# Expert stage of a hybrid transformer block: combining products one pair later, the first pair's rows fetched alone, the last pair evacuated in halves

## The chip, the cores and the metric

The kernel runs as one program on one core of a Trainium2 chip. The metric is the device time of one execution in microseconds (us). A profiled execution gives the trace: its span runs from the first to the last instruction, and a little time lies around the span.

## The reference, cut to what matters

The program computes a first block with two mixers, then a second block with a sparse-attention mixer and a mixture of experts, then a norm. Only the mixture of experts is touched here. Each of 512 tokens is routed to 2 of 32 experts; every expert is a gated two-layer network.

```python
def run(args):                                   # xb: the rows of one expert
    xb, e = args
    gate, up = jnp.split(xb @ w_gate_up[e], 2, axis=-1)
    return (jax.nn.silu(gate) * up) @ w_down[e]
...
y = jax.ops.segment_sum(y_buf[dest] * w_s[:, None].astype(h.dtype), tok_s, num_segments=n_tok)
```

`w_gate_up[e]` is 1024 x 512 and `w_down[e]` is 256 x 1024, in 32-bit floats: 3 MB for each expert, all of which has to be read once.

## The kernel before, in words

All of this is in `moe`. **Routing** works on 128 partitions by 4 token tiles: `rs` is the inverse norm of a token, `rk` its rank within its expert, `Wd` its weight. `wr` holds, for each pair of experts, the weights, `rs` and the token numbers, split into a high and a low part (a copy on ScalarE, a subtraction on VectorE: `split`, lines 328 and 329). `rkT` is `rk` transposed.

**Slots.** Each expert has 64 slots, so a pair of experts fills 128 partitions. There are 16 pairs, j = 0 to 15, in 8 groups of two, g = 0 to 7.

- `prepare(g)` builds a 0/1 matrix `P` on VectorE (L1956), multiplies it with `wr` (L1961) to get the token number and the weights of each slot, turns the numbers into indices `ix` (L1966), and gathers the rows of the tokens from device memory with two indirect DMAs on GpSimd (L1969), one for each pair. `s3`, `w` and `r` (L1972 to L1976) are small sums and copies on GpSimd.
- `turn(j)` transposes the gathered rows in two halves of four 128 x 128 blocks on TensorE (L1994) through one PSUM bank, `ga`, and scales them into `Xs`, alternating ScalarE and VectorE (L1983, L1981).
- `gate_up(j)` multiplies with the weights of the two experts (L2011). Each expert uses a 64-column half of the array, and the two halves run side by side when their calls alternate. ScalarE evacuates the result into `G` (L2013).
- `act(j)` transposes `G` (L2020) and applies the gate (L2022 to L2025), giving `H`.
- `down(j)` multiplies `H` with the second weights into `dn` (L2034), again one half of the array for each expert, and evacuates 128 x 1024 numbers as a high part `yh` on ScalarE (L2037) and a low part `yl` on VectorE (L2038). It also builds `PT`, the matrix that sends slots back to tokens (L2041, L2043).
- `combine(g)` is a generator of eight groups (4 token tiles x 2 column halves). Each group has four products, `yh` and `yl` of two pairs (L2052), in one of two `cb` banks, and one addition into `acc` on VectorE (L2055).

**Order.** For pair j the loop issues `gate_up(j)`, the first half of `turn(j + 1)`, `down(j - 1)`, the second half of `turn(j + 1)`, four combining groups, and `act(j)`. The groups of pairs 2g and 2g + 1 begin in the iteration whose `down` is that of pair 2g + 1. This order is only a priority: a planner, which runs the program against its own costs, fixes the order of the instructions on each engine, and it may put later work in where earlier work isn't ready by its reckoning. Within an engine the order so fixed is then kept on the chip. `tc.issue_after(x)` puts the instructions of a block behind `x` on `x`'s own engine.

**Weights** are streamed by SyncE's queue into a ring of buffers of 1 MB, about 12 of them in this stage; a buffer is loaded again when its last product is done.

**End.** `down(15)` is followed by all eight groups of the last two pairs, and `last_norm` squares on ScalarE, scales on VectorE (L2097) and stores. `overflow` handles experts with over 64 tokens: its few small VectorE instructions (L2108 to L2120) count them, and its loop does not run here.

Of the kernel before, what the change touches and what calls it, by code (L numbers as in the profile page):

```python
# [10 lines left out]
FT = mybir.dt.float32  # L11
FR = mybir.dt.float32r
BF = mybir.dt.bfloat16
I32 = mybir.dt.int32
AF = mybir.ActivationFunctionType
# [5 lines left out]
D = 1024  # L21
# [304 lines left out]
def split(k, raw, hi, lo, lo_eng=None):  # L326
    nc = k.nc
    nc.scalar.copy(hi, raw)
    (lo_eng or nc.vector).tensor_tensor(lo, raw, hi.bitcast(FT), OP.subtract)
# [1457 lines left out]
def moe(k, A, C, out, ctx, mhp, mh, ml):  # L1787
# [36 lines left out]
    with tc.tile_pool(name="mo1", bufs=2, reuse_waits="tile") as wk, tc.tile_pool(name="mo1x", bufs=1, reuse_waits="tile") as xp, \  # L1824
# [99 lines left out]
            nc.tensor.matmul(rp[:, 4], oneb, asg[:, u], start=(u == 0), stop=(u == 3))  # L1924

        nc.vector.tensor_scalar(rk, asg, -1000.0, 1000.0, op0=OP.mult, op1=OP.add)
        nc.vector.tensor_tensor(rk, rk, rp[:, 0:4], OP.add)
        nc.vector.tensor_copy(cnt, rp[:, 4])
        d, r = tiny(1, "d"), tiny(1, "r")
        nc.vector.tensor_tensor(d, m2, m1, OP.subtract)  # L1930
# [4 lines left out]
        nc.vector.tensor_tensor(Wd, o1, r.to_broadcast(b32), OP.mult)  # L1935
        nc.vector.tensor_tensor(o2, o2, d.to_broadcast(b32), OP.mult)
        nc.vector.tensor_tensor(Wd, Wd, o2, OP.add)
        wp = Wd.rearrange("p t (j e) -> p t j e", e=2)
        split(k, wp, wr[:, :, :, 0:4:2], wr[:, :, :, 1:4:2])
        rsb = rs[:, :, None].to_broadcast([128, 4, N_PAIR])  # L1940
        split(k, rsb, wr[:, :, :, 4], wr[:, :, :, 5])
        tr = pp.tile([128, 512], FT, name="pg", bufs=2)
        for i in range(4):
            nc.tensor.transpose(tr[0:32, i * 128:i * 128 + 128], rk[:, i], k.ident)
# [4 lines left out]
    with tc.tile_pool(name="mo2", bufs=2, reuse_waits="tile") as wk, tc.tile_pool(name="mo2y", bufs=1, reuse_waits="tile", side="right") as yp, \  # L1949
# [3 lines left out]
        def prepare(g):  # L1953

            P = wk.tile([128, 4, 4, 64], FR, name="P", bufs=1)
            nc.vector.tensor_tensor(P, rk[:, :, 4 * g:4 * g + 4, None].to_broadcast([128, 4, 4, 64]),  # L1956
                                    iota[:, None, None, :].to_broadcast([128, 4, 4, 64]), OP.is_equal)
            sp = pp.tile([128, 2, 8], FT, name="cb", bufs=2)
            for j in range(2):
                for t in range(4):  # L1960
                    nc.tensor.matmul(sp[:, j], P[:, t, 2 * j:2 * j + 2].rearrange("p e s -> p (e s)"),  # L1961
                                     wr[:, t, 2 * g + j], start=(t == 0), stop=(t == 3))
            s8 = wk.tile([128, 2, 8], FT, name="s8")
            nc.vector.tensor_copy(s8, sp)
            ix = wk.tile([128, 2], I32, name="ix")
            nc.vector.tensor_copy(ix, sp[:, :, 6])  # L1966
            for j in range(2):
                x = XG[2 * g + j] = wk.tile([128, D], FT, name="xg", bufs=3)
                nc.gpsimd.indirect_dma_start(out=x, out_offset=None, in_=xd[:, :],  # L1969
                                             in_offset=bass.IndirectOffsetOnAxis(ap=ix[:, j:j + 1], axis=0))  # L1970
            s3 = wk.tile([128, 2, 3], FT, name="s3")
            nc.gpsimd.tensor_tensor(s3, s8[:, :, 0:6:2], s8[:, :, 1:6:2], OP.add)  # L1972
            w, r = (wk.tile([128, 2], FT, name=n, bufs=3) for n in ("sw", "sr"))
            for i, a in enumerate((slice(0, 64), slice(64, 128))):
                nc.gpsimd.tensor_copy(w[a], s3[a, :, i])
            nc.gpsimd.tensor_copy(r, s3[:, :, 2])  # L1976
            SW[g] = (w, r)

        def scaled(x, v, kk):
# [21 lines left out]
        def gate_up(j):  # L2001

            g, i = divmod(j, 2)
            ps = pp.tile([128, 512], FT, name="gu", bufs=2)
            xs = Xs.pop(j)
            for c in range(2):
                ws = [k.W.get_raw() for _ in HALF]
                for a in range(4):
                    kk = 4 * c + a
                    for o, w in zip(HALF, ws):  # L2010
                        nc.tensor.matmul(ps[o], xs[:, kk, o], w[:, a], start=(kk == 0), stop=(kk == 7))  # L2011
            G[j] = wk.tile([128, 512], FT, name="G")
            nc.scalar.activation(G[j], ps, AF.Copy, scale=SW[g][1][:, i:i + 1])  # L2013

        def act(j):

            tp = pp.tile([128, 4, 128], FT, name="T")
            x = G.pop(j)
            for f in range(4):
                nc.tensor.transpose(tp[:, f], x[:, 256 * (f // 2) + f % 2:256 * (f // 2) + 256:2], k.ident)  # L2020
            th = wk.tile([128, 2, 128], FT, name="th")
            nc.scalar.activation(th, tp[:, 0:2], AF.Tanh, scale=0.5)  # L2022
            nc.vector.scalar_tensor_tensor(th, th, 1.0, tp[:, 0:2], op0=OP.add, op1=OP.mult)
            H[j] = wk.tile([128, 2, 128], FT, name="H")
            nc.vector.scalar_tensor_tensor(H[j], th, 0.5, tp[:, 2:4], op0=OP.mult, op1=OP.mult)  # L2025

        def down(j):
            ps = pp.tile([128, 2, 512], FT, name="dn")
            h = H.pop(j)
            ws = [k.W.get_raw() for _ in HALF]  # L2030
            for a in range(2):
                for i in range(2):
                    for o, w in zip(HALF, ws):
                        nc.tensor.matmul(ps[o, i], h[:, a, o], w[:, a, 512 * i:512 * i + 512], start=(a == 0), stop=(a == 1))  # L2034
            w = SW[j // 2][0][:, j % 2:j % 2 + 1]
            yh, yl = (yp.tile([128, 2, 512], FR, name=n, bufs=3) for n in ("yh", "yl"))
            nc.scalar.activation(yh, ps, AF.Copy, scale=w)  # L2037
            nc.vector.scalar_tensor_tensor(yl, ps, w, yh.bitcast(FT), op0=OP.mult, op1=OP.subtract)  # L2038
            Y[j] = (yh, yl)
            b = pp.tile([128, 512], FT, name="cb", bufs=2)  # L2040
            nc.tensor.matmul(b, sel[:, 2 * j:2 * j + 2].rearrange("p e s -> p (e s)"), rkT, start=True, stop=True)  # L2041
            PT[j] = yp.tile([128, 512], FR, name="PT", bufs=3)
            nc.vector.tensor_scalar(PT[j], b, col64, None, op0=OP.is_equal)  # L2043

        def combine(g):
            for t in range(4):
                for i in range(2):
                    ps = pp.tile([128, 512], FT, name="cb", bufs=2)
                    n = 0
                    for j in (2 * g, 2 * g + 1):  # L2050
                        for y in Y[j]:
                            nc.tensor.matmul(ps, PT[j][:, t * 128:t * 128 + 128], y[:, i], start=(n == 0), stop=(n == 3))  # L2052
                            n += 1
                    a = acc[:, t, 512 * i:512 * i + 512]
                    nc.vector.tensor_tensor(a, a, ps, OP.add)  # L2055
                    yield

        def steps(g, n):
            for _ in range(n):
                next(g, None)  # L2060
# [4 lines left out]
        for j in range(N_PAIR):  # L2065
            g, i = divmod(j, 2)
            if i == 0 and g + 1 < NG:
                prepare(g + 1)
            gate_up(j)
            nxt = turn(j + 1) if j + 1 < N_PAIR else iter(())  # L2070
            steps(nxt, 1)
            if j:
                down(j - 1)
            if i == 0 and g:
                comb = combine(g - 1)
            steps(nxt, 2)
            steps(comb, 4)
            act(j)
        for _ in comb:
            pass  # L2080
        down(N_PAIR - 1)
        for _ in combine(NG - 1):
            pass


    with tc.tile_pool(name="mo3", bufs=2, reuse_waits="tile") as wk:
        gf = wk.tile([128, D], FT, name="gf", bufs=1)
        nc.scalar.dma_start(gf, A["norm_final_2"].rearrange("(o d) -> o d", o=1).to_broadcast([128, D]))

        def last_norm():  # L2090
            ss, rf = wk.tile([128, 4], FT, name="ss", bufs=1), wk.tile([128, 4], FT, name="rf", bufs=1)
            for t in range(4):
                s = wk.tile([128, D], FT, name="s", bufs=4)
                nc.scalar.activation(s, acc[:, t], AF.Square, accum_out=ss[:, t:t + 1])
                nc.vector.tensor_scalar(ss[:, t:t + 1], ss[:, t:t + 1], 1.0 / D, EPS, op0=OP.mult, op1=OP.add)
                nc.gpsimd.tensor_tensor(rf[:, t:t + 1], ss[:, t:t + 1], k.mhalf, OP.pow)
                nc.vector.scalar_tensor_tensor(s, acc[:, t], rf[:, t:t + 1], gf, op0=OP.mult, op1=OP.mult)  # L2097
                nc.sync.dma_start(out[0, t * 128:t * 128 + 128], s)
        last_norm()
        overflow(k, A, rt, cm, rk, Wd, rs, cnt, xd, acc, last_norm)  # L2100


def overflow(k, A, rt, cm, rk, Wd, rs, cnt, xd, acc, last_norm):

    nc, tc = k.nc, k.tc
    iota, ids, tok = cm[:, 0:64], cm[:, 193:201], cm[:, 201:205]
    x = rt.tile([128, 32], FT, name="ovx")
    nc.vector.tensor_scalar(x, cnt, 64.0, None, op0=OP.is_gt)  # L2108
    for j in range(2, 8):
        nc.vector.scalar_tensor_tensor(x, cnt, 64.0 * j, x, op0=OP.is_gt, op1=OP.add)  # L2110
    ci = x
# [125 lines left out]
```

## Time and profile before

| what | us |
|---|---|
| three runs | 2397.03, 2403.26, 2406.48 (median 2403.26) |
| the profiled execution | 2399.58 |
| its span | 2397.8 |
| busy: TensorE (PE) / VectorE (DVE) / ScalarE (ACT) / GpSimd (POOL) | 2258.6 / 1536.0 / 1068.5 / 710.5 |
| from the first store of normed rows to the first product with expert weights | 2043.5 to 2068.3 |
| first product with expert weights to the last addition | 2068.3 to 2386.5 |

A busy PE is one with a matmul under way by a modelled end; it is not PE at its peak. In the rows below PE is TensorE's matmuls and L with a number is a line of the kernel. "x16" counts records: one call of `gate_up` or `down` gives two, one combining product gives one.

### The profile page before, as it was taken

The numbers are of one execution on the slowest core, as the hardware profiler recorded it, in microseconds if no ns is written. First come the engines' busy times: TensorE is split into PE (matmuls) and PEld (weight loads), VectorE is DVE, ScalarE is ACT, GpSimd is POOL, SyncE is SP. The second block draws the span as 40 slices with busy tenths as digits, with TensorE's granted clock in tenths as the row PEclk, the third lists the DMA queues.
The fourth block names the chain that finished last, engine by engine and source line by source line (L and its number), as shares of the span: only waits on it lengthen the run. The fifth ranks groups of instructions, "written<-read, shape, count | busy, mean of one in ns | idle before, by whom it ended". The sixth has DMA issues, their size and how long they took to land. (4 is left out here: it accounts for less than half of the span.)

```text
span 2397.8 us, 37215 instructions
## 1 busy us (share of the span) xinstructions
PE 2258.6 (94%) x14396; PEld 1844.0 (77%) x14396; DVE 1536.0 (64%) x2845; ACT 1068.5 (45%) x2164; POOL 710.5 (30%) x709
## 2 busy tenths in 40 slices
PE   7999999998999989999999989899999999799997
PEld 6989999997889888888898869887666667344333
DVE  7778764537985587787767744678678554433333
ACT  5666654433344466566656644435444432121111
POOL 3455540115642333333323325432011021101000
PEclk9999999999999899999999989898999999799998
DMA  6333322223127422111111225532121336699871
GB/s 225 125 108 111 113 93 89 88 71 105 56 85 217 142 62 71 53 54 53 58 49 54 71 89 173 179 82 64 62 75 53 115 103 236 254 423 372 330 299 45
DMA packets 242061, 306.19 MB, mean 128 GB/s; under 512 B 20648, under 2 KB 208436, under 8 KB 233306
## 3 DMA queue, kind: packets, MB, share of 16 engines
q1 hardware_dynamic: 203328, 245.90, 30.6%
q10 hardware_dynamic: 33002, 32.64, 4.5%
q0 software_dynamic: 5552, 25.25, 2.9%
q8 instruction: 114, 1.87, 0.3%
q14 instruction: 65, 0.53, 0.1%
HBM read 278.19 MB, written 25.58 MB: 127 GB/s over the span
## 5 line engine op out<-in xcount | busy, mean ns | idle before, releaser
L263 POOL TENSOR_TENSOR wlo<-wraw,whi 128x1024 fp32r<-128x1024 f32 (+1 forms) x91 | 181.0, 1997 | 479.2 <-ACT whi L282 346.7
L263 DVE TENSOR_TENSOR wlo<-wraw,whi 128x1024 fp32r<-128x1024 f32 (+2 forms) x201 | 225.5, 1135 | 148.7 <-ACT whi L282 141.1
L282 ACT CAST whi<-wraw 128x1024 fp32r<-128x1024 f32 x198 | 206.0, 1047 | 169.9 <-PE ps L813 50.2
L811 PE MATMUL ps<-xh,whi 128*128 128x264 f32 x1024 | 214.0, 286 | 3.4 <-ACT hTd L584 3.0
L813 PE MATMUL ps<-xl,whi 128*128 128x264 f32 x1024 | 213.9, 286 | 0.0
L815 PE MATMUL ps<-xh,wlo 128*128 128x264 f32 x1024 | 211.8, 285 | 0.0
L811 PE MATMUL pj<-xh,whi 128*128 128x512 f32 (+2 forms) x544 | 193.9, 359 | 5.0 <-DVE rr L1193 4.6
L815 PE MATMUL pj<-xh,wlo 128*128 128x512 f32 (+2 forms) x544 | 191.2, 354 | 0.5 <-DVE wlo L263 0.5
L813 PE MATMUL pj<-xl,whi 128*128 128x512 f32 (+2 forms) x544 | 191.4, 354 | 0.0
L811 PEld LDWEIGHTS ps<-xh,whi 128*128 128x128 f32 x1024 | 160.5, 189 | 5.8 <-ACT hTd L584 4.0
L813 PEld LDWEIGHTS ps<-xl,whi 128*128 128x128 f32 x1024 | 161.2, 189 | 1.6 <-issue 1.3
L815 PEld LDWEIGHTS ps<-xh,wlo 128*128 128x128 f32 x1024 | 160.8, 189 | 1.2 <-issue 0.8
L813 PE MATMUL pj<-vx,whi 128*128 128x256 f32 (+1 forms) x480 | 136.6, 286 | 0.0
L1302 ACT ACTIVATE p<-S,mx 128x528 f32<-128x528 f32 x128 | 89.6, 702 | 77.5 <-DVE mx L1300 42.6
L811 PEld LDWEIGHTS pj<-xh,whi 128*128 128x128 f32 x544 | 104.8, 193 | 19.9 <-DVE rr L1193 6.0
L815 PEld LDWEIGHTS pj<-xh,wlo 128*128 128x128 f32 x544 | 104.0, 192 | 13.7 <-DVE wlo L263 0.7
L813 PEld LDWEIGHTS pj<-xl,whi 128*128 128x128 f32 x544 | 104.4, 193 | 12.6
L2011 PE MATMUL gu<-wraw,Xs 128*64 128x512 f32 x400 | 112.1, 626 | 0.0
L1300 DVE TENSOR_REDUCE mx<-S 128x1 f32<-128x528 f32 x128 | 88.9, 700 | 13.6 <-PE S L1299 12.2
L2055 DVE TENSOR_TENSOR acc<-acc,cb 128x512 f32<-128x512 f32 x64 | 43.1, 684 | 79.6 <-PE cb L2052 79.4
L813 PEld LDWEIGHTS pj<-vx,whi 128*128 128x128 f32 x480 | 91.6, 191 | 0.0
L1298 PE MATMUL S<-ks,qh 128*128 128x264 f32 x256 | 71.9, 301 | 11.9 <-ACT p L1302 11.7
(662 smaller groups left out, 6482.7 us busy)
## 6 DMA issues: line engine op xcount, KB each, us to landing
wraw<-in_w_gate_up_dram SPq DMA_DIRECT2D x50, 1024.0 KB
wraw<-in_hy_w_in_dram SPq DMA_DIRECT2D x32, 1024.0 KB
wraw<-in_da_w_in_dram SPq DMA_DIRECT2D x32, 1024.0 KB
wraw<-in_hy_w_out_dram SPq DMA_DIRECT2D x16, 1024.0 KB
wraw<-in_da_w_out_dram SPq DMA_DIRECT2D x16, 1024.0 KB
wraw<-in_w_down_dram SPq DMA_DIRECT2D x14, 1024.0 KB
wraw<-in_w_in_dram SPq DMA_DIRECT2D x20, 512.0 KB
whi<-in_w_down_dram SPq DMA_DIRECT2D x18, 512.0 KB
```

What stands on the lines that cost most here:

```text
L263: eng.tensor_tensor(l, r, h.bitcast(FT), OP.subtract)
L282: nc.scalar.copy(hf, vf)
L811: nc.tensor.matmul(ps[i], wh[:, kk, fsl], xh[:, kk, c], start=f, stop=False)
L813: nc.tensor.matmul(ps[i], wh[:, kk, fsl], xl[:, kk, c], start=False, stop=False)
L815: nc.tensor.matmul(ps[i], wl[:, kk, fsl], xh[:, kk, c], start=False, stop=l)
L1298: nc.tensor.matmul(S[:, i, 0:TH], qh[:, qs], ks[:, c], start=True, stop=False)
L1300: nc.vector.tensor_reduce(mx[:, m:m + 1], S[:, :, 0:TH], AX.XY, OP.max, negate=True)
L1302: nc.scalar.activation(p.rearrange("p (a b) -> p a b", a=2), S[:, :, 0:TH], AF.Exp, bias=mx[:, m:m + 1], accum_out=sm[:, m:m + 1])
L2011: nc.tensor.matmul(ps[o], xs[:, kk, o], w[:, a], start=(kk == 0), stop=(kk == 7))
L2055: nc.vector.tensor_tensor(a, a, ps, OP.add)
```

## The change

- `prepare(0)` builds `P`, the slot products, the index and the gather for pair 0 alone, then those of pair 1. The later groups stay whole. In `prepare` the gathers come before the copy to `s8`, and for g = 0 the small sums run on VectorE instead of GpSimd.
- The split of `rs` is put behind the last rank instruction on VectorE. The first `overflow` instruction is put behind `act(4)`.
- In iteration j four combining groups are issued right behind the last product of `gate_up(j)`, before `down(j - 1)`; the generator is replaced after that, so a group of pairs is combined one iteration later. `turn(j + 1)` is issued whole after `down(j - 1)`.
- `down` builds `PT` first and finishes one column half of `dn` before the other; for the last pair each half is evacuated by itself.
- `last_combine` starts the sums of the last two pairs with pair 14's products in six banks (`gu` twice, `ga`, `T`, `cb` twice) and, once it is free, in `dn`; pair 15's products then finish them.

```diff
-        nc.vector.tensor_tensor(rk, rk, rp[:, 0:4], OP.add)
+        last_rank = nc.vector.tensor_tensor(rk, rk, rp[:, 0:4], OP.add)
...
+        rsb = rs[:, :, None].to_broadcast([128, 4, N_PAIR])
+        with tc.issue_after(last_rank.ins):
+            split(k, rsb, wr[:, :, :, 4], wr[:, :, :, 5])
         wp = Wd.rearrange("p t (j e) -> p t j e", e=2)
         split(k, wp, wr[:, :, :, 0:4:2], wr[:, :, :, 1:4:2])
-        rsb = rs[:, :, None].to_broadcast([128, 4, N_PAIR])
-        split(k, rsb, wr[:, :, :, 4], wr[:, :, :, 5])
...
+            for js in ((0,), (1,)) if g == 0 else ((0, 1),):
+                c = slice(2 * js[0], 2 * js[-1] + 2)
+                n = c.stop - c.start
+                nc.vector.tensor_tensor(P[:, :, c], rk[:, :, 4 * g + c.start:4 * g + c.stop, None].to_broadcast([128, 4, n, 64]),
+                                        iota[:, None, None, :].to_broadcast([128, 4, n, 64]), OP.is_equal)
+                for j in js:
+                    for t in range(4):
+                        nc.tensor.matmul(sp[:, j], P[:, t, 2 * j:2 * j + 2].rearrange("p e s -> p (e s)"),
+                                         wr[:, t, 2 * g + j], start=(t == 0), stop=(t == 3))
+                c = slice(js[0], js[-1] + 1)
+                nc.vector.tensor_copy(ix[:, c], sp[:, c, 6])
+                for j in js:
+                    x = XG[2 * g + j] = wk.tile([128, D], FT, name="xg", bufs=3)
+                    nc.gpsimd.indirect_dma_start(out=x, out_offset=None, in_=xd[:, :],
+                                                 in_offset=bass.IndirectOffsetOnAxis(ap=ix[:, j:j + 1], axis=0))
...
+            eng = nc.gpsimd if g else nc.vector
+            eng.tensor_tensor(s3, s8[:, :, 0:6:2], s8[:, :, 1:6:2], OP.add)
...
         def down(j):
...
+            last = j == N_PAIR - 1
+            for i in range(2):
+                for a in range(2):
+                    for o, wt in zip(HALF, ws):
+                        nc.tensor.matmul(ps[o, i], h[:, a, o], wt[:, a, 512 * i:512 * i + 512], start=(a == 0), stop=(a == 1))
+                if last or i:
+                    c = slice(i, i + 1) if last else slice(0, 2)
+                    nc.scalar.activation(yh[:, c], ps[:, c], AF.Copy, scale=w)
+                    nc.vector.scalar_tensor_tensor(yl[:, c], ps[:, c], w, yh[:, c].bitcast(FT), op0=OP.mult, op1=OP.subtract)
...
+        def last_combine():
+            banks = []
+            for n, b in (("gu", 2), ("gu", 2), ("ga", 1), ("T", 1), ("cb", 2), ("cb", 2)):
+                ps = pp.tile([128, 512], FT, name=n, bufs=b)
+                t, i = divmod(len(banks), 2)
+                add(ps, t, i, N_PAIR - 2, True, False)
+                banks.append(ps)
+            ps = None
+            for t in range(4):
+                if t == 3:
+                    ps = pp.tile([128, 2, 512], FT, name="dn")
+                    banks += [ps[:, i] for i in range(2)]
+                    for i in range(2):
+                        add(banks[6 + i], t, i, N_PAIR - 2, True, False)
+                for i in range(2):
+                    add(banks[2 * t + i], t, i, N_PAIR - 1, False, True)
+                    a = acc[:, t, 512 * i:512 * i + 512]
+                    nc.vector.tensor_tensor(a, a, banks[2 * t + i], OP.add)
...
-            gate_up(j)
+            done = gate_up(j)
             nxt = turn(j + 1) if j + 1 < N_PAIR else iter(())
-            steps(nxt, 1)
+            with tc.issue_after(done):
+                steps(comb, 4)
             if j:
                 down(j - 1)
             if i == 0 and g:
                 comb = combine(g - 1)
-            steps(nxt, 2)
-            steps(comb, 4)
-            act(j)
+            steps(nxt, 3)
+            hidden = act(j)
+            if j == 4:
+                late = hidden
         for _ in comb:
             pass
         down(N_PAIR - 1)
-        for _ in combine(NG - 1):
-            pass
+        last_combine()
...
+    with tc.issue_after(late):
+        nc.vector.tensor_scalar(x, cnt, 64.0, None, op0=OP.is_gt)
```

## Rows read from the trace of the kernel before

**Rows 1.** Busy time of each engine in two stretches of the expert stage.
```profile
core 0: us, PE busy (x) PEld busy (x) DVE busy (x) ACT busy (x) POOL busy (x), PEclk, DMA share, GB/s
2081.08:2210.43 129.35, 129.35 (x579) 55.70 (x577) 48.27 (x91) 26.02 (x53) 11.86 (x19) 1.00 0.99 399
2210.43:2366.97 156.54, 147.82 (x580) 58.38 (x579) 51.89 (x93) 26.09 (x49) 6.31 (x12) 0.98 0.69 261
```

**Rows 2.** TensorE's waits in the second stretch: total us, times, longest.
```profile
PE cb L2052 <- ACT yh L2037: 4.8, 4, 1.2
PE cb L2052 <- DVE yl L2038: 2.3, 4, 0.6
```

**Rows 3.** Chain of waits at two of four stalls: start us, us, what.
```profile
2211.89 3.15 PE dn L2034 x13
...
2215.51 1.12 ACT yh L2037
2216.66 1.29 DVE yl L2038
...
2218.93 5.00 PE gu L2011 x14
...
2303.57 5.27 PE gu L2011 x14
```

**Rows 4.** Chain of waits: an uncut block of products, and a cut one.
```profile
2077.57 3.58 PE gu L2011 x16
...
2272.71 2.04 PE cb L2052 x8
2274.74 1.00 PE gu L2011 x2
2275.75 1.13 PE cb L2052 x4
2276.87 3.58 PE gu L2011 x14
```

**Rows 5.** Timeline of VectorE in the routing: start us, us, what, idle before.
```profile
2046.69 0.28 DVE L329 TENSOR_TENSOR wr<-rs,wr 128x64 fp32r<-128x64 f32 x1 [0.88 <-ACT wr L328]
2046.88 0.17 DVE L1897 TENSOR_TENSOR ge<-L,gm 128x16 f32<-128x16 f32 x1
...
2053.40 1.23 DVE L1956 TENSOR_TENSOR P<-rk,cm 128x1024 fp32r<-128x1024 f32 x1
...
2057.31 0.15 DVE L1966 CAST ix<-cb 128x2 int32<-128x2 f32 x1
```

**Rows 6.** Timeline of TensorE around the first gather.
```profile
2054.97 1.87 PE L1961 MATMUL cb<-wr,P 128*128 128x8 f32 x8 [0.51 <-DVE wr L329]
...
2063.36 1.97 PE L1994 MATMUL gu<-ident,xg 128*128 128x128 f32 x8 [2.25 <-DMA xg<-xd,ix]
```

**Rows 7.** Timeline of GpSimd around the first gather.
```profile
2057.48 1.18 POOL L1972 TENSOR_TENSOR s<-s 128x6 f32<-128x6 f32 x1 [12.64 <-DVE ix L1966]
2058.83 1.13 POOL L1969 DMA_INDIRECT xg<-xd,ix  x1 [0.17 <-DVE ovc L2115]
```

**Rows 8.** Groups by line in the expert stage: busy us, mean ns of one.
```profile
L2055 DVE TENSOR_TENSOR acc<-acc,cb 128x512 f32<-128x512 f32 x64 | 43.1, 684 | 79.6 <-PE cb L2052 79.4
...
L2037 ACT ACTIVATE yh<-dn,sw 128x1024 fp32r<-128x1024 f32 x16 | 17.8, 1115 | 97.7 <-PE dn L2034 97.7
...
L2013 ACT ACTIVATE G<-gu,sr 128x512 f32<-128x512 f32 x16 | 11.0, 688 | 80.5 <-PE gu L2011 80.5
```

**Rows 9.** Chain of waits at the end of the stage.
```profile
2369.15 3.67 PE dn L2034 x16
...
2376.90 6.39 PE cb L2052 x16
...
2388.51 1.28 DVE s L2097
```

**Rows 10.** Timeline of TensorE: two halves of one `turn`.
```profile
2331.95 0.65 PE L1994 MATMUL ga<-ident,xg 128*128 128x128 f32 x4
...
2334.29 0.66 PE L1994 MATMUL ga<-ident,xg 128*128 128x128 f32 x4 [0.69 <-DVE Xs L1981]
```

More of the change, by code (lines that the diff above doesn't have):

```diff
@@ L1955, in prepare @@
             P = wk.tile([128, 4, 4, 64], FR, name="P", bufs=1)
-            nc.vector.tensor_tensor(P, rk[:, :, 4 * g:4 * g + 4, None].to_broadcast([128, 4, 4, 64]),
-                                    iota[:, None, None, :].to_broadcast([128, 4, 4, 64]), OP.is_equal)
             sp = pp.tile([128, 2, 8], FT, name="cb", bufs=2)
[L1959 to L1962, printed above, removed]
@@ L1963, in prepare @@
             s8 = wk.tile([128, 2, 8], FT, name="s8")
-            nc.vector.tensor_copy(s8, sp)
[L1965 to L1970, printed above, removed]
+            ix = wk.tile([128, 2], I32, name="ix")
@@ L1971, in prepare @@
+            nc.vector.tensor_copy(s8, sp)
             s3 = wk.tile([128, 2, 3], FT, name="s3")
-            nc.gpsimd.tensor_tensor(s3, s8[:, :, 0:6:2], s8[:, :, 1:6:2], OP.add)
+            eng = nc.gpsimd if g else nc.vector
+            eng.tensor_tensor(s3, s8[:, :, 0:6:2], s8[:, :, 1:6:2], OP.add)
             w, r = (wk.tile([128, 2], FT, name=n, bufs=3) for n in ("sw", "sr"))
             for i, a in enumerate((slice(0, 64), slice(64, 128))):
-                nc.gpsimd.tensor_copy(w[a], s3[a, :, i])
@@ L1976, in prepare @@
-            nc.gpsimd.tensor_copy(r, s3[:, :, 2])
+                eng.tensor_copy(w[a], s3[a, :, i])
+            eng.tensor_copy(r, s3[:, :, 2])
             SW[g] = (w, r)
@@ L2010, in gate_up @@
                     for o, w in zip(HALF, ws):
-                        nc.tensor.matmul(ps[o], xs[:, kk, o], w[:, a], start=(kk == 0), stop=(kk == 7))
+                        mm = nc.tensor.matmul(ps[o], xs[:, kk, o], w[:, a], start=(kk == 0), stop=(kk == 7))
             G[j] = wk.tile([128, 512], FT, name="G")
             nc.scalar.activation(G[j], ps, AF.Copy, scale=SW[g][1][:, i:i + 1])
+            return mm.ins
         def act(j):
@@ L2024, in act @@
             H[j] = wk.tile([128, 2, 128], FT, name="H")
-            nc.vector.scalar_tensor_tensor(H[j], th, 0.5, tp[:, 2:4], op0=OP.mult, op1=OP.mult)
+            return nc.vector.scalar_tensor_tensor(H[j], th, 0.5, tp[:, 2:4], op0=OP.mult, op1=OP.mult).ins
         def down(j):
[L2028 to L2039, printed above, removed]
             b = pp.tile([128, 512], FT, name="cb", bufs=2)
@@ L2043, in down, with add @@
             nc.vector.tensor_scalar(PT[j], b, col64, None, op0=OP.is_equal)
+            ps = pp.tile([128, 2, 512], FT, name="dn")
+            h = H.pop(j)
+            ws = [k.W.get_raw() for _ in HALF]
+            w = SW[j // 2][0][:, j % 2:j % 2 + 1]
+            yh, yl = (yp.tile([128, 2, 512], FR, name=n, bufs=3) for n in ("yh", "yl"))
+            last = j == N_PAIR - 1
[7 more added lines that the diff above has]
+                    nc.vector.scalar_tensor_tensor(yl[:, c], ps[:, c], w, yh[:, c].bitcast(FT), op0=OP.mult, op1=OP.subtract)
+            Y[j] = (yh, yl)
+        def add(ps, t, i, j, start, stop):
+            for n, y in enumerate(Y[j]):
+                nc.tensor.matmul(ps, PT[j][:, t * 128:t * 128 + 128], y[:, i], start=(start and n == 0), stop=(stop and n == 1))
         def combine(g):
@@ L2048, in combine @@
                     ps = pp.tile([128, 512], FT, name="cb", bufs=2)
-                    n = 0
                     for j in (2 * g, 2 * g + 1):
-                        for y in Y[j]:
-                            nc.tensor.matmul(ps, PT[j][:, t * 128:t * 128 + 128], y[:, i], start=(n == 0), stop=(n == 3))
-                            n += 1
+                        add(ps, t, i, j, j % 2 == 0, j % 2 == 1)
                     a = acc[:, t, 512 * i:512 * i + 512]
@@ L2056, in combine @@
                     yield
+        def last_combine():
[8 more added lines that the diff above has]
+                if t == 3:
+                    ps = pp.tile([128, 2, 512], FT, name="dn")
+                    banks += [ps[:, i] for i in range(2)]
[5 more added lines that the diff above has]
+                    nc.vector.tensor_tensor(a, a, banks[2 * t + i], OP.add)
         def steps(g, n):
@@ L2099, in moe, with overflow @@
         last_norm()
-        overflow(k, A, rt, cm, rk, Wd, rs, cnt, xd, acc, last_norm)
-def overflow(k, A, rt, cm, rk, Wd, rs, cnt, xd, acc, last_norm):
+        overflow(k, A, rt, cm, rk, Wd, rs, cnt, xd, acc, last_norm, late)
+def overflow(k, A, rt, cm, rk, Wd, rs, cnt, xd, acc, last_norm, late):
     nc, tc = k.nc, k.tc
@@ L2107, in overflow @@
     x = rt.tile([128, 32], FT, name="ovx")
-    nc.vector.tensor_scalar(x, cnt, 64.0, None, op0=OP.is_gt)
+    with tc.issue_after(late):
+        nc.vector.tensor_scalar(x, cnt, 64.0, None, op0=OP.is_gt)
     for j in range(2, 8):
```

## Prediction

> **What bounds the kernel now.** I first read the busy time by stretches [rows 1]. The two rows cut the expert stage at the transposes of G of pair 0, pair 8 and pair 15. Both hold the same number of TensorE records, yet the first takes 129.35 us for eight pairs (16.2 us each) and the second 156.54 us for seven (22.4 us each). TensorE is the bound in both: VectorE and ScalarE are under 40% busy, and the DMA engines, full in the first stretch (0.99), are at 0.69 in the second. So the second stretch loses time that no transfer explains. The waits of TensorE there name part of it: four times a combining product waited for `yh` and then for `yl` [rows 2]. The chain of waits shows one such place: the down products of a pair end, 1.12 us of ScalarE and 1.29 us of VectorE pass, and only then does TensorE go on, at half the granted clock for a while [rows 3]. The rest is in how the order cuts the streams of products [rows 4]. Ahead of the stage, the routing is a single chain of small instructions that ends in the first gather [rows 5 to 7]. Behind it, the last combine and the norm form another [rows 9].
>
> **The change, part by part.**
>
> A, the first gather. Four things leave the chain before it. (1) VectorE sat 0.88 us until ScalarE had copied `rs`, and the subtraction held the next instruction another 0.19 us [rows 5]: 1.07 us, of which 0.28 come back when the subtraction is issued behind the ranks; 0.79 us net. (2) Half of the 1.23 us for `P` [rows 5] and half of the 1.87 us of slot products [rows 6] fall behind the gather: 0.61 and 0.93 us. (3) The slot products end at 2054.97 + 1.87 = 2056.84 and `ix` starts at 2057.31, behind `overflow` work and the copy to `s8`: of 0.47 us I leave 0.1. (4) `ix` ends at 2057.46 and the gather starts at 2058.83, because GpSimd did the sum `s3` first [rows 7]: of 1.37 us I leave 0.1. The sum is 0.79 + 0.61 + 0.93 + 0.37 + 1.27 = 3.97 us. The second half of `P` may come ahead of `ix` on VectorE (0.61 us), or `rkT` may, which is about as long; both bring the gain down to 2.7. I take 3.6, nearer the upper end, since the planner sets both behind `ix` in priority. The first transpose starts when the rows land [rows 6], so a gather that is earlier starts the stage earlier by the same amount. The moved VectorE work (the small sums of g = 0 and `overflow`'s counting) costs nothing as long as VectorE is under 40% busy [rows 1]; on the path it would be about 1.5 us.
>
> A sum of six elements on GpSimd took 1.18 us [rows 7] while VectorE ran the next `P` (from 2057.38, right behind `ix`). By the Trainium skill (SBUF — State Buffer, section "SBUF: two separate sides") the two engines take a shared pair of ports in turn, and a VectorE instruction with two SBUF inputs shuts GpSimd out until it ends. That speaks against this part: the second half of `P` would hold up the gather that the change brings forward. The 1.18 us agrees with the rule; by it A would be 3.97 − 0.61 = 3.4, and the gain 0.2 us smaller.
>
> B, the four stalls. From the end of the down products (2211.89 + 3.15 = 2215.04) to the next product with expert weights (2218.93) there are 3.89 us, in which four combining products ran, 1.13 us in a stream [rows 3, 4]: 2.76 us lost. The other three stalls, reckoned alike, lose 2.57, 2.63 and 2.57. That is 10.5 us; the waits alone are 7.1 [rows 2], and I keep both ends. After the change the groups issued behind `gate_up(j)` belong to pairs whose `yh` and `yl` were made an iteration earlier, behind at least a whole `gate_up`, two blocks of 3.58 us [rows 4], against 2.4 us of evacuation [rows 3]. So this wait goes; what is late next is the transposes (E). I take 10.5.
>
> C, the clock. Two of the four stalls were followed by a block of 5.00 and 5.27 us, where the same block takes 3.58 [rows 3, 4]; I take these 1.42 + 1.69 = 3.1 us, bounds 0 and 3.1.
>
> D, the cuts. A block of 16 records takes 3.58 us. Where a combining group is put between its first call and the rest, the first two records take 1.00 and the other fourteen still 3.58, since one half of the array stands empty beside the lone call [rows 4]: 1.0 us for each cut. I count 17 pieces of two in the chain, 5 in the first stretch and 12 in the second. With groups tied behind `gate_up(j)` and ready at once, fewer should be left over to be put into other blocks, but the planner decides. Bounds 0 and 17 us; I take 6, a third, because the ties keep groups from coming between the products of the same `gate_up` and not from the `down` behind it.
>
> E, the transposes. `turn(j + 1)` was issued around `down(j - 1)`; now both halves come behind it, and the second needs the bank that the first fills. In one place the two halves stand 2.34 us apart, 0.65 of it work [rows 10]: up to 1.69 us uncovered for each of 15 pairs, 25.4 us. The cover is the transposes of G, the combining groups (1.1 us each, [rows 4]) and whatever the planner finds ready; the 0.69 us of that row is the only wait of its kind in the trace. Bounds 0 and 25.4, and I take a cost of 2.
>
> F, the end. From the end of `down(15)` (2369.15 + 3.67 = 2372.82) to the end of the last scaling (2388.51 + 1.28 = 2389.79) there are 16.97 us, with 6.39 us for 16 combining products at half the clock [rows 9]; at full clock eight take 2.04 [rows 4]. After the change TensorE has pair 14's twelve products to do at once, 3.06 us at full clock, while the halves are evacuated; with two more products the first addition starts some 3.6 us behind `down`. Then VectorE is the bound: 8 additions of 0.684 [rows 8] and 4 scalings of 1.28 [rows 9] are 10.6 us. That is 14.2 in place of 16.97: 2.8 us. An evacuation in halves costs 2 x 0.688 in place of 1.115 us on ScalarE [rows 8], but the first half lies under the second half of `down`. Bounds 0 (the additions wait for the halves in turn) and 4.9 (pair 14's products run before `down(15)` ends, and the first addition starts at about 1.5). I take 2.8.
>
> Building `PT` first, the column-half order of `down`, and the larger number of VectorE instructions cost nothing while TensorE is the bound.
>
> Sum: 3.6 + 10.5 + 3.1 + 6 − 2 + 2.8 = 24.0 us off the profiled execution's 2399.58, so 2375.6. The profiled execution lies 3.7 us under the median of the three runs, and I put the level between them, 1.8 us up: **2377.4 us**.
>
> **The rivals.**
>
> (i) Weights bind. The DMA engines are already full in the first stretch, at 399 GB/s [rows 1], and a pair needs six buffers of 1 MB, 15.8 us; without combining a pair would take less on TensorE. The change has one more such pair at the start. For it: the 0.99. Against it: only about one pair is affected, since with combining a pair already takes 16.2 us. Four groups of 1.02 us [rows 4] are a pair's share, so without them it takes about 12.1 us on TensorE and waits 15.8 − 12.1 = 3.7: 2381.
>
> (ii) The cuts get no fewer, or the early pairs are cut like the late ones: 12 for 7 pairs would be 27 for 16, 10 more than the 17 now. No gain of 6 and 10 us more: 2393. For it: the planner cut the second stretch by its own costs, not by the chip's. Against it: the ties.
>
> (iii) The transposes show at every pair, once: 25.4 us instead of 2, so 2377.4 + 23.4 = 2401: no difference. For it: both halves are now behind `down`. Against it: a single wait of this kind so far [rows 10].
>
> (iv) Slower: the same bank holds TensorE up twice for each pair, once between the halves of `turn` and once more before the products of the next `gate_up` that need the second half. 2 x 1.69 x 15 = 50.7 us, against 26.0 of gains without E: 2426. It decides from 26 / 15 = 1.7 us a pair, and from 2.5 us the loss is over 0.5%. For it: nothing is issued any more between the second half and `gate_up` but the transposes of G. Against it: the needed blocks are the later half of `gate_up`, 3.58 us on [rows 4].
>
> **How the numbers follow.** About 0.5% or 12 us is what a measurement here can tell from no change, so faster is under 2391. Chances: forecast 0.60, (i) 0.06, (ii) 0.13, (iii) 0.12, (iv) 0.09. Faster is the first two and half of (ii), 0.73; the same the other half of (ii) and (iii), 0.18; slower (iv), 0.09. The low end takes the upper bounds of A, B, F and 13 of D's 17 at no cost in E: 4.0 + 10.5 + 3.1 + 13 + 4.9 = 35.5, or 2366; I go to 2363 for level. The high end, 2398, takes in (i), (ii) and the milder part of (iii). The forecast's own range is 2366 to 2388.
>
> **What would show it.** A: the first transposes start near 2059.8 rather than 2063.4, and no GpSimd sum stands before the first gather. B and C: no wait of a combining product for `yh` or `yl` before the last pair, and a granted clock of 1.00 from pair 1 to the last `down`. D: fewer pieces of two in the chain. E: waits of `ga` for `Xs` in TensorE's list, over 10 us in all if (iii) holds. F: about 14 us from the end of `down(15)` to the last scaling. The prediction is wrong if the order that the planner finds cuts the blocks more often, or if the transposes come late.

## The result, and the profile after

The changed kernel takes 2363.74 us (median of four runs, 2360.36 to 2371.49) against 2401.17 us of the kernel before on the same chip (four runs, 2397.03 to 2406.48). The ratio is 0.9847, with a 95% interval of 0.9814 to 0.9881: 37 us faster, where 24 were forecast. The time is just above the low end of the range (2363 to 2398) and below the forecast's own range (2366 to 2388).

The same two stretches as in [rows 1], cut at the transposes of G of pairs 0, 8 and 15, in the kernel after:

```profile
core 0: us, PE busy (x) PEld busy (x) DVE busy (x) ACT busy (x) POOL busy (x), PEclk, DMA share, GB/s
2076.30:2198.41 122.11, 121.80 (x569) 54.44 (x567) 49.63 (x109) 27.44 (x55) 10.99 (x17) 1.00 1.02 419
2198.41:2323.76 125.35, 124.83 (x563) 56.18 (x563) 48.19 (x86) 25.50 (x47) 6.53 (x14) 1.00 0.82 326
```

The first stretch lost 7.2 us and the second 31.2 (156.54 to 125.35), with nearly the same number of records. TensorE still bounds both, and its granted clock is 1.00 throughout.

TensorE's list of waits from 2045 to 2390 us (total, times, longest), to be held against [rows 2]:

```profile
PE dn L2057 <- DVE acc L2088: 1.0, 1, 1.0
...
PE gu L2000 <- DMA xg<-xd,ix: 0.6, 1, 0.6
PE gu L2017 <- ACT Xs L1989: 0.5, 1, 0.5
...
PE T L2027 <- ACT G L2019: 0.3, 1, 0.3
```

No wait for `yh` or `yl` is left, and none of the transposes for `Xs`. The chain of waits still has cut blocks beside uncut ones, as in [rows 4], but only 7 pieces of two. The chain before has 16 of them, 5 in the first stretch and 11 in the second; the 17 of the prediction is one too many.

```profile
2197.48 1.00 PE dn L2048 x2
2198.48 0.68 PE T L2027 x4
2199.16 1.85 PE cb L2057 x8
...
2201.01 3.58 PE dn L2048 x14
2204.90 3.58 PE gu L2017 x16
2208.49 3.43 PE dn L2048 x16
2211.92 3.43 PE gu L2017 x16
```

At the start, the timeline of VectorE (against [rows 5]):

```profile
2049.36 1.29 DVE L1963 TENSOR_TENSOR P<-rk,cm 128x512 fp32r<-128x512 f32 x2
...
2051.96 0.16 DVE L1970 CAST ix<-cb 128x1 int32<-128x1 f32 x1 [0.52 <-PE cb L1967]
```

of GpSimd (against [rows 7]; the last line is the small sum of g = 1):

```profile
2052.95 1.13 POOL L1973 DMA_INDIRECT xg<-xd,ix  x1 [11.29 <-DVE ix L1970]
...
2058.82 0.22 POOL L1978 TENSOR_TENSOR s<-s 128x6 f32<-128x6 f32 x1
```

and of TensorE (against [rows 6]):

```profile
2057.74 1.97 PE L2000 MATMUL gu<-ident,xg 128*128 128x128 f32 x8 [0.63 <-DMA xg<-xd,ix]
...
2062.87 9.33 PE L2017 MATMUL gu<-wraw,Xs 128*64 128x512 f32 x32
```

And the chain at the end, against [rows 9]:

```profile
2326.55 1.87 PE dn L2048 x8
2328.42 2.04 PE cb L2057 x8
2330.46 0.91 PE gu L2057 x4
2331.36 0.45 PE ga L2057 x2
2331.82 0.45 PE T L2057 x2
2332.27 1.83 PE cb L2057 x8
...
2335.59 1.87 PE dn L2048 x8
...
2339.51 1.42 DVE acc L2088 x3
```

The two halves of `down(15)` (`dn` x8 twice) stand 7.2 us apart, with pair 14's products between them.

**A common scale.** The routing's first instruction on VectorE (the copy of `rs`, L1876) starts at 2043.36 us before and at 2040.19 after, although the instructions ahead of it are the same, in the same order but for four products of TensorE; over the fourteen profiled executions of this study it lies anywhere from 2040.19 to 2055.42. So stages are compared from that instruction (t0) to the end of the last scaling; each number is from one profiled execution. "Expert products" is the time from each product of `gate_up` or `down` to the next record, waits left out and without `gate_up(0)`, whose time depends on the clock at the start of the stage; "combining" is the same for the combining products; "waits" are TensorE's gaps of over 0.15 us from the transposes of G of pair 0 on. A run is a series of calls of `gate_up` and `down` with no other product between, counted in the order that the planner wrote for TensorE, and an odd run has an odd number of calls. (The traces show one even run fewer than that order, except in e7 and e10 to e12, where the two agree.)

| kernel | median us, ratio | stage | first expert product | expert products | combining | waits | runs / odd |
|---|---|---|---|---|---|---|---|
| before | 2401.17 | 346.4 | 24.9 | 189.1 | 74.1 | 11.1 | 78 / 38 |
| after | 2363.74, 0.9847 | 310.0 | 22.7 | 172.5 | 64.4 | 2.3 | 48 / 18 |
| e1 later, no tie | 2404.35, 1.0006 | 343.4 | 24.9 | 188.0 | 72.4 | 11.2 | 79 / 42 |
| e2 tie, not later | 2399.44, 0.9991 | 343.3 | 25.2 | 187.2 | 70.7 | 13.0 | 75 / 38 |
| e3 later and tied | 2379.46, 0.9903 | 327.1 | 24.9 | 183.1 | 66.4 | 5.6 | 63 / 32 |
| e4 whole new loop | 2370.52, 0.9854 | 309.8 | 24.9 | 172.4 | 65.3 | 1.9 | 47 / 18 |
| e5 after, old end | 2369.10, 0.9879 | 308.4 | 22.7 | 172.4 | 65.3 | 2.4 | 47 / 18 |
| e6 after, old start | 2371.20, 0.9881 | 310.6 | 25.0 | 172.5 | 64.4 | 1.8 | 48 / 18 |
| e7 after, order fixed | 2357.00, 0.9825 | 299.4 | 20.2 | 162.8 | 65.3 | 3.3 | 33 / 0 |
| e8 after, halves in turn | 2414.91 (one run) | 359.6 | 21.6 | 222.6 | 64.7 | 2.7 | 53 / 30 |
| e9 after, no tie | 2403.55, 0.9999 | 343.2 | 23.0 | 189.4 | 71.2 | 10.7 | 79 / 42 |
| e10 e7, odd cuts | 2370.99, 0.9873 | 315.3 | 20.2 | 175.7 | 65.8 | 3.9 | 46 / 26 |
| e11 e7, even cuts | 2361.95, 0.9837 | 304.3 | 20.2 | 164.7 | 65.9 | 3.9 | 46 / 0 |
| e12 e7, old end | 2355.79, 0.9805 | 298.4 | 20.1 | 162.6 | 66.2 | 3.5 | 32 / 0 |

Ratios are to runs of the kernel before on the same chip.

### The profile page after: what moved, and what is told of

Same layout as the page of the kernel before. It is cut to its first block, busy times and chain, and to the rows that moved or that the text cites. A ratio compares the mean times of both kernels' runs of the same rounds, so it can differ in the third digit from the quotient of the medians.

```text
span 2358.6 us, 37218 instructions
## 1 busy us (share of the span) xinstructions
PE 2227.2 (94%) x14396; PEld 1841.4 (78%) x14396; DVE 1535.9 (65%) x2852; ACT 1070.8 (45%) x2165; POOL 707.9 (30%) x705
## 5 line engine op out<-in xcount | busy, mean ns | idle before, releaser
L815 PE MATMUL pj<-xh,wlo 128*128 128x512 f32 (+2 forms) x544 | 189.1, 351 | 0.4 <-DVE wlo L263 0.4
L2017 PE MATMUL gu<-wraw,Xs 128*64 128x512 f32 x400 | 97.3, 609 | 0.0
L1298 PE MATMUL S<-ks,qh 128*128 128x264 f32 x256 | 71.6, 300 | 11.9 <-ACT p L1302 11.7
L1656 ACT ACTIVATE P<-S,mx 128x128 f32<-128x128 f32 (+3 forms) x96 | 50.3, 530 | 70.0 <-PE pt L1673 56.6
```

Source lines behind the costliest of these rows:

```text
L815: nc.tensor.matmul(ps[i], wl[:, kk, fsl], xh[:, kk, c], start=False, stop=l)
L1298: nc.tensor.matmul(S[:, i, 0:TH], qh[:, qs], ks[:, c], start=True, stop=False)
L1656: nc.scalar.activation(p[:, m, 0:n], S[:, m, 0:n], AF.Exp, bias=mx[:, m:m + 1], accum_out=sm[:, m:m + 1])
L2017: mm = nc.tensor.matmul(ps[o], xs[:, kk, o], w[:, a], start=(kk == 0), stop=(kk == 7))
```

## The experiments

**e1 to e4: which part of the loop.** e1 is the kernel before with the groups issued one pair later and nothing else; e2 ties them behind `gate_up(j)` in their old place; e3 does both; e4 moves `turn` behind `down` as well, with the old gather, `down` and end. (`done` is in e3 and e4 what it is in e2.)

```diff
             steps(nxt, 1)                        # e1
+            steps(comb, 4)
             if j:
                 down(j - 1)
...
             steps(nxt, 2)
-            steps(comb, 4)
```
```diff
-            gate_up(j)                           # e2
+            done = gate_up(j)
...
-            steps(comb, 4)
+            with tc.issue_after(done):
+                steps(comb, 4)
```
```diff
-            steps(nxt, 1)                        # e4; e3 keeps the two lines of nxt
+            with tc.issue_after(done):
+                steps(comb, 4)
             if j:
                 down(j - 1)
...
-            steps(nxt, 2)
-            steps(comb, 4)
+            steps(nxt, 3)
```

> The kernel before, with the four combining groups one pair later, ahead of down, and nothing tied; turn stays around down. Theory 1 (waits and lone halves): the waits for yh and yl and the half clock behind them go, 13.6 us, but in the order written for this program 42 runs of expert products have an odd number of calls and so leave half of the array empty once (38 before, 18 in the changed kernel, 0.43 us each), in 79 runs in all (78 and 48, 0.16 us each for the switch): 2401.2 - 13.6 + 1.7 + 0.2 = 2389.5. Theory 2 (the later combining is the gain, by its waits and its freedom): the whole middle gain of some 30 us, 2371.

> The kernel before, with the combining groups at their old place, only tied behind the last product of gate_up; they still follow the down of their own pair. Theory 1: 38 odd runs of 75, as before; the waits for yh and yl stay: 2400.7. Rival (the tie is what keeps the blocks whole): some 15 us less, 2386.

> The kernel before, with the groups one pair later and tied; the first half of turn still ahead of them, the rest behind down. Theory 1: 32 odd runs of 63: 13.6 + 6 x 0.43 + 15 x 0.16 = 18.6 us less, 2382.6. Theory 2: 2371, the same as with turn moved.

> The kernel before with the whole new loop (groups later and tied, turn whole behind down), but the old first gather, the old down and the old end. Theory 1: 18 odd runs of 47: 13.6 + 20 x 0.43 + 31 x 0.16 = 27.2 us less, 2374, so the move of turn is worth 8 to 9 us more than the same loop without it. Rival (term E of the prediction: the transposes lose their cover): slower than the loop with turn around down, by up to 25 us.

Neither half does anything alone: e1 has a ratio of 1.0006 (0.9988 to 1.0025) and e2 0.9991 (0.9975 to 1.0007), though the stage is some 3 us shorter in both. Every expectation for e1 missed; e2, e3 and e4 came within 4 us of theory 1 (2400.7, 2382.6 and 2374). Its list of waits still holds

```profile
PE cb L2052 <- ACT yh L2037: 6.0, 5, 1.2
PE cb L2052 <- DVE yl L2038: 2.9, 5, 0.6
```

(four in the loop and one behind `down(15)`). Issued later but free, the groups are hoisted by the planner to where they were. In e2 they can't be hoisted, but they belong to the pair whose `down` has just ended, so they wait (5.4 and 2.9 us in the same two rows of its list). Both together give 0.9903 (0.9876 to 0.9930), and the move of `turn` takes it to 0.9854 (0.9820 to 0.9888): the loop alone has all of the change's gain, 36.6 us of the stage against 36.4. The rival that the moved transposes would cost time fell; they gave 8.9 us by the medians and 17.2 in the stage of the profiled executions. The intervals of e3 and e4 overlap, so the stage carries this: the four kernels with this loop (after, e4, e5 and e6) lie within 2.2 us of one another there.

**e5 and e6: the end and the start undone.** e5 is the kernel after with the last evacuation whole and `combine(NG - 1)` behind `down(15)`; e6 has the old routing, `prepare` and `overflow`.

```diff
-            last = j == N_PAIR - 1               # e5
+            last = False
...
-        last_combine()
+        for _ in combine(NG - 1):
+            pass
```
```diff
-            for js in ((0,), (1,)) if g == 0 else ((0, 1),):   # e6, core
...
-            eng = nc.gpsimd if g else nc.vector
-            eng.tensor_tensor(s3, s8[:, :, 0:6:2], s8[:, :, 1:6:2], OP.add)
+            nc.gpsimd.tensor_tensor(s3, s8[:, :, 0:6:2], s8[:, :, 1:6:2], OP.add)
```

> The changed kernel with the old end: the last two pairs combined by the ordinary groups, the last down evacuated whole. Term F of the prediction: 2.8 us are lost, 2366.5, and from the end of the last down to the last scaling there are again about 17 us. From the two traces (16.97 and 12.7 us) I expect 4.2, 2368. Rival: the end is hidden behind the norm on VectorE and nothing is lost, 2363.7.

> The changed kernel with the old routing order, the old prepare and overflow's first instruction untied. Term A of the prediction: 3.6 us are lost, 2367.3. By the traces, counted from the first instruction of the routing on VectorE to the first product with expert weights, the loss is 2.2, 2366. Rival: the stage is paced by the weights behind it and nothing is lost, 2363.7.

The ratios, 0.9879 (0.9843 to 0.9915) and 0.9881 (0.9845 to 0.9918), overlap that of the kernel after, so medians settle neither. By the stages neither expectation came true (4.2 and 2.2 us lost): with the old end it is 1.6 us shorter than after, with the old start 0.6 us longer. Part of both is `gate_up(0)`, the same products at another clock: to the next record 9.26 us at a granted clock of 0.75 in the kernel after, 8.46 at 0.83 in e5, and 8.17 at 0.86 in e6, which so gets back 1.1 of the 2.3 us by which its first expert product is later. The new end takes 12.7 us from the end of `down(15)` to the last scaling where e5 takes 19.2, but `down(15)` ends 7.3 us later (261.2 against 253.8 us behind the transposes of pair 0), since pair 14's products stand ahead of its second half.

**e7: the whole order written out.** Every TensorE step of the loop is tied to the last product of the step before it: `prepare`, `gate_up(j)`, two groups, half of `turn`, a third group, the transposes of `act(j)`, the fourth group, `down(j - 1)`, the other half of `turn`.

```diff
-            done = gate_up(j)
+            tied(lambda: gate_up(j))
             nxt = turn(j + 1) if j + 1 < N_PAIR else iter(())
-            with tc.issue_after(done):
-                steps(comb, 4)
+            tied(lambda: next(comb, None))
+            tied(lambda: next(comb, None))
+            tied(lambda: next(nxt, None))
+            tied(lambda: next(comb, None))
+            hidden, _ = tied(lambda: act(j))
+            tied(lambda: next(comb, None))
             if j:
-                down(j - 1)
+                tied(lambda: down(j - 1))
...
```

> The changed kernel with the order of TensorE's work in the pair loop written out by ties: gate_up, two combining groups, first half of the next turn, a group, the transposes of G, a group, down, second half of the next turn. No run of expert products has an odd number of calls any more (18 in the changed kernel), and there are 33 runs (48). Theory 1: 18 x 0.43 + 15 x 0.16 = 10.1 us less than the changed kernel, 2353.6. Rival (the planner's freedom hid waits that a fixed order shows): the second half of turn and the transposes of G wait for ScalarE and VectorE, up to 1.7 us a pair, 2380.

2357.00 us, 0.9825 (0.9789 to 0.9862); the first theory is 3.4 us off, the rival 23. The interval overlaps that of the kernel after, but the stage is 10.6 us shorter, and 9.7 of that are expert products.

**e8: the two halves of the array in turn.** The four calls of one expert, then the four of the other.

```diff
-                for a in range(4):
-                    kk = 4 * c + a
-                    for o, w in zip(HALF, ws):
+                for o, w in zip(HALF, ws):
+                    for a in range(4):
+                        kk = 4 * c + a
```

> The changed kernel with the calls of gate_up in another order: four for one expert, then four for the other, so that the two halves of the array work side by side only at the three seams of sixteen calls. If a lone call costs 0.86 us and a pair side by side the same (theory 1), gate_up takes 13 x 0.86 = 11.2 us instead of 7.2, 4.0 to 4.3 us more for 16 pairs: 2363.7 + 67 = 2431. If the halves do not work side by side and the cuts cost something else, the time does not change, 2364.

2414.91 us in one run. Its chain shows a block of sixteen records at 5.35 us where the alternating order takes 3.58 [rows 4]:

```profile
2076.26 5.35 PE gu L2017 x16
2081.62 0.67 PE T L2027 x4
2082.29 5.35 PE gu L2017 x16
```

The rival fell: the halves do work side by side. The price, 50 us of expert products, was under the theory's 67.

**e9: the change without its tie.**

```diff
-            with tc.issue_after(done):
-                steps(comb, 4)
+            steps(comb, 4)
```

> The kernel after, with one thing undone: the four groups of combining products stand behind the next pair's gate_up as in the change, but without the tie to its last product. Theory (the tie is what holds them there; without it the planner hoists them, as in e1): TensorE waits again about 8 times for yh and yl, the expert products fall back into some 79 runs, 42 of them odd, and the stage is about 32 us longer than in the kernel after (343 of e1 less what the first gather keeps, against 310): 2395 us. Rival (the moved transposes alone undo the cuts, and the tie is worth only the waits of some 9 us): 2373 us.

2403.55 us, 0.9999 (0.9982 to 1.0016): one line takes back everything. The two waits of [rows 2] are back to the digit, in its list of waits:

```profile
PE cb L2057 <- ACT yh L2051: 4.8, 4, 1.2
PE cb L2057 <- DVE yl L2052: 2.3, 4, 0.6
```

and the second stretch takes what it took before [rows 1]; its busy time by stretches:

```profile
2216.74:2372.21 155.47, 146.75 (x579) 58.74 (x579) 51.23 (x91) 25.52 (x47) 6.16 (x12) 0.99 0.67 255
```

The stage is 33.2 us longer than after (32 expected), so the rival (2373) fell; the median is 8.6 us above the 2395 expected, of which t0 explains part (2049.95).

**e10 and e11: the price of a cut.** From e7, the fourth group of 13 pairs is moved into `down`, behind its first call (e10, runs of one and seven) or behind its second (e11, runs of two and six).

```diff
+                        if mid and calls == 1:       # e11: == 2
+                            with tc.issue_after(dm.ins):
+                                group = next(mid, None)
+                        with tc.issue_after(group or bm):
                             dm = nc.tensor.matmul(ps[o, i], h[:, a, o], wt[:, a, 512 * i:512 * i + 512], start=(a == 0), stop=(a == 1))
+                        calls += 1
```

> The kernel e7, whose order on TensorE is fixed and has no odd run of expert products, with one group of combining products of each of 13 pairs moved behind the first call of down, so that down falls into a run of one call and one of seven. Theory 1 (a call whose other half of the array stands idle takes nearly the time of a pair of calls, about 1.0 us): 13 x 1.0 = 13 us more than e7, 2370 us; the two records of the lone call show about 1.0 us. Rival (what costs is each switch between expert and combining products, odd or even): the same as e11, some 2 us, 2359 us.

> As e10, but with the group behind the second call of down, so that down falls into runs of two and six, as many runs as in e10 and none odd. Theory 1: nothing but the switches, 13 x 0.15 = 2 us more than e7, 2359 us. Rival (the number of runs costs, not that they are odd): as long as e10, by theory 1 about 2370 us.

The timeline of TensorE in e10, one pair:

```profile
2208.18 1.07 PE L2055 MATMUL dn<-wraw,H 128*64 128x512 f32 x2
2209.18 0.50 PE L2066 MATMUL cb<-yh,PT 128*128 128x512 f32 x1
...
2210.31 3.65 PE L2055 MATMUL dn<-wraw,H 128*64 128x512 f32 x14
2213.89 0.66 PE L2001 MATMUL ga<-ident,xg 128*128 128x128 f32 x4
```

and in e11, the same pair:

```profile
2202.74 1.08 PE L2055 MATMUL dn<-wraw,H 128*64 128x512 f32 x4
2203.75 0.50 PE L2066 MATMUL cb<-yh,PT 128*128 128x512 f32 x1
...
2204.88 2.79 PE L2055 MATMUL dn<-wraw,H 128*64 128x512 f32 x12
2207.61 0.66 PE L2001 MATMUL ga<-ident,xg 128*128 128x128 f32 x4
```

Two records alone take 1.07 us and four take 1.08; fourteen take 3.65 and twelve 2.79. From the first of these products to the transposes behind them are 5.71 us in e10 and 4.87 in e11: 0.84 us for a cut at an odd place. Times 13 that is 10.9 us, and 11.0 lie between their expert products (175.7 and 164.7). The stages differ by 11.1 us and the medians by 9.0; the intervals of the ratios (0.9832 to 0.9914, 0.9801 to 0.9874) overlap, so the trace carries this verdict. The rival, that only the number of runs counts, fell. An even cut adds 1.9 us of expert products for 13 more runs, 0.15 each. e11 is 4.9 us longer in the stage than e7, more than the 2 expected; 2.3 of it stand in the transposes of G, which e10 shares, and why is open.

**e12: the best parts.** e7 with the old end, by the same edit as e5.

> The kernel e7 with the end of the kernel before: the last pair's result evacuated whole, and the last groups of combining products all behind the last down. Theory (the new end only moves pair 14's products ahead of the last down, which comes as much later): within 2 us of e7, 2357 us. Rival (the shorter way from the last down to the last scaling is a gain by itself, 16.3 to 11.5 us): some 5 us slower than e7, 2362 us.

2355.79 us, 0.9805 (0.9765 to 0.9844), with a stage of 298.4 against 299.4 in e7: the new end gains nothing here either and loses 1.0 us. (The way from the last `down` to the last scaling takes 12.7 us in e7, not the 11.5 of the expectation, and 16.3 in e12.) Its interval overlaps those of e7 and of the kernel after, but the order it shares with e7 makes the stage 11.6 us shorter than after.

## Why the prediction was right in its direction, step by step

The mechanism was right: time left the second stretch, the waits for `yh` and `yl` and the half clock went, and blocks are cut less. Several terms were mis-sized, two of them by much, and E had the wrong sign. The time is inside the range because its low end took 13 us for D and no cost for E. The stage's 36.4 us, by the table and the rows, against the terms of the sum:

| step | forecast | shown |
|---|---|---|
| A, first gather | 3.6 | 1.6 at the transposes of pair 0 |
| B, four stalls | 10.5 | 8.4: 7.1 of waits, 1.3 in the products of the stalls |
| C, half clock | 3.1 | clock 1.00, so about 3.1 |
| D, cuts | 6 | 13.5 of expert products, and about 4.8 of combining |
| E, transposes | −2 | no wait; about +1.5 in transposes and small products |
| F, end | 2.8 | 3.6 at the end, but the new end itself loses about 1 |

The combining products take 9.7 us less. 1.3 of it lie at the four stalls, where four products took 1.26 to 1.59 us in place of 1.13. 3.6 lie in the 32 products of the last two pairs: 11.7 us before, where sixteen of them took 6.39 us [rows 9] at a granted clock of 0.59, and 8.1 after, at 1.00. The other 4.8 are put down to fewer breaks and not shown by a run of their own: the combining products stand in 35 series in place of 55, and one at the edge of a series takes 0.30 to 0.33 us to the next record where one inside takes 0.23 to 0.26.

**A was mis-sized.** The first transposes start 17.55 us behind t0 in place of 20.00, which is 2.45 us and less than the lower bound of 2.7. Two steps failed. The first is "the planner sets both behind `ix` in priority": it put both halves of `P` (1.29 us) ahead of the first slot products, so the 0.61 us for half of `P` did not come. The second is "of 1.37 us I leave 0.1": no sum stands ahead of the gather any more, but GpSimd starts it 0.83 us after the end of `ix`, so 0.54 us came in place of 1.27. VectorE was idle in that time, and the chain calls 0.79 us of it `issue`; why is open. The first expert product is 2.2 us earlier. Then `gate_up(0)` took 9.33 us at a granted clock of 0.76, against 8.71 at 0.81 before, and at the transposes of pair 0 the gain is 1.6; over the whole stage e6 finds 0.6. The rule of the Trainium skill (SBUF — State Buffer, section "SBUF: two separate sides") was not put to this test, since the second half of `P` was over by then; it agrees with the small sum of g = 1, which took 0.22 us with VectorE idle beside it where the same sum of g = 0 took 1.18 [rows 7].

**B and C were right in kind.** The waits for `yh` and `yl` at the four stalls, 7.1 us, are gone, and the granted clock, 0.72 and 0.68 in the two long blocks of [rows 3], is 1.00 throughout after the change. But B was reckoned from a line that is not the end of the down products. In the chain before they go on behind the 13 records of [rows 3]:

```profile
2211.89 3.15 PE dn L2034 x13
2215.04 0.01 PE gu L2011
2215.05 0.44 PE dn L2034
```

It is the same at the other three stalls, so each is 0.44 us shorter than taken, and reckoned from there the four lose 8.7 us in place of 10.5 (8.4 by the records themselves, as in the table). What the forecast did not see is that B hangs on the tie: e1 and e9 show that the later place alone moves nothing.

**D was the term that was mis-sized most.** The forecast priced a cut well (1.0 us; e10 shows 0.84) and counted too few of them: the pieces of two in the chain, of which it let a third go. What counts is every run of expert products, and every odd one more: by e10 and e11, 0.15 us for a run and 11.0 / 26 = 0.42 for an odd run. From 78 runs, 38 odd, to 48 and 18, that is 4.5 + 8.4 = 12.9 us, and with C's 3.1 it makes 16.0; 16.6 were measured. From e3 to e4 the same prices give 2.4 + 5.9 = 8.3 against 10.7, from after to e7 9.8 against 9.7, and from before to e1 1.8 more where 1.1 less were measured: right to some 3 us. The rule of the Trainium skill that tiles work independently of each other (TensorEngine Tiling (Array Packing), section "Key Properties") agrees with e8's 5.35 against 3.58 us and e10's 1.07 us; the price of an unpaired call stands in the rows alone.

**E had the wrong sign.** "The second needs the bank that the first fills" is true, but no such wait is in the list after: transposes of G and combining groups cover it. And the move removed 14 odd runs (e3 to e4), since the first half of `turn` no longer stands between `gate_up` and `down`. Rivals (iii) and (iv) fall with it, and so does (ii). Rival (i), weights: the DMA share rose to 1.02 in the first stretch, and TensorE's list has no wait for them.

**F failed.** From the end of `down(15)` to the last scaling are 12.7 us, less than the 14.2 forecast, but the upper bound's condition, "pair 14's products run before `down(15)` ends", came with a cost the step left out: they delay `down(15)` by more than that gains. The 3.6 us that the end did gain (1.8 of waits and 3.6 of products, less 1.7 behind the last product and 0.1 of other waits) come from the loop: e4 has the old end, and its stage is as short as that of the kernel after. The new end alone loses 1.0 us between e12 and e7, and 0.8 between e5 and after once `gate_up(0)` is left out.

## What to carry to other kernels

Where a planner fixes the order, the place in the program is a wish: look in the trace for where the work landed, and tie it when the place matters. When two halves of the array work side by side, count the runs of their calls and keep each even; the breaks between streams gave more here (18 us, 13.5 of them in the expert products) than the waits that the profile names (9). Work pulled ahead of the last block is no gain when the bound engine does both.

## What the runs showed of the hardware that was not expected

- A lone call on one half of the array takes the time of a pair of calls, one on each half (1.07 us for two records, 1.08 for four). But a series of calls on one half is not twice as long as the alternating one: 5.35 against 3.58 us for sixteen records.
- The time ahead of this stage, with the same instructions in nearly the same order, differs by up to 15 us between executions (t0 from 2040.19 to 2055.42 us), which is more than several of the parts of this change are worth.
